# A hybrid Hyena and attention layer on one core: all gate pairs in the Strassen stage, hyena branch products beside the attention

## The chip, the core and the metric

The kernel runs on one core of a Trainium2 chip. The core has a matrix engine (TensorE, PE in the profile, with its weight loads as PEld), VectorE (DVE), ScalarE (ACT), GpSimd (POOL) and a queue engine (SP) that here only issues transfers. Matrix products land in eight banks of a small accumulator memory (PSUM) and are taken from there by VectorE or ScalarE. The metric is the device time of one execution in microseconds (us), lower is better.

## What is computed

One layer of an encoder, 512 tokens of width 2048, in float32. A normalised input goes through one wide projection; its columns feed a Hyena branch (short convolutions, long convolution by transforms), an attention branch (8 query heads, 2 key/value heads) and two gates. The gated branches are added, projected and followed by a feed-forward block of width 5632.

```python
h = rms_norm(x, mix_norm_g)
proj = h @ w_in
u_h, q, k, v, g = jnp.split(proj, [c0, c1, c2, c3], axis=-1)
...
g_h, g_a = jnp.split(jax.nn.sigmoid(g + b_gate), 2, axis=-1)
merged = g_h * (y_h @ w_br_hyena) + g_a * (y_a @ w_br_attn)
x = x + merged @ w_out
h2 = rms_norm(x, ffn_norm_g)
return x + (jax.nn.silu(h2 @ w_ffn_gate) * (h2 @ w_ffn_up)) @ w_ffn_down
```

`y_h` comes from `u_h`, `y_a` from q, k and v. The gates have 2 x 2048 output channels: 16 tiles of 128 for `g_h` and 16 for `g_a`. Pair m is tile m of both. The branch products `y_h @ w_br_hyena` and `y_a @ w_br_attn` also have 16 tiles of 128 channels each, with a depth of 1024 (8 blocks).

## The kernel before

Activations lie with channels on the 128 partitions and the 512 tokens along the free side; a tile of 128 channels is `[128, 512]`. To keep float32 accuracy every operand is split into a high and a low part (ACT copies the high part, DVE subtracts to get the low one), and a plain product is three matmuls (`mm3`): high by high, high by low, low by high.

**Weights** come from one packed array `wpk` in the order of use (`weight_blocks`, L61), in tiles of eight 128x128 blocks. `wblk` (L162) loads a tile through SP's queue, and ACT (`wh`, L175) and DVE (`wl`, L176) split it; two raw and three split tiles can be in flight. `group` (L186) makes one output tile of 128 channels from n input tiles: n steps of three matmuls, each followed by a call of `step()`. A gate tile has 16 steps, a branch product 8.

**Side work.** `step()` advances a queue of generators, one at a time (`side`). A generator emits a piece of work and yields the number of steps until its next piece. The attention is such a generator, `attend_gen` (L676): it waits `Q_WAIT` (25 and 26) steps, transposes four heads, then goes through eight units `u` in which `scores` (matmuls, softmax on DVE and ACT), `turn` (transposes of the probabilities into `pt`, split by ACT and DVE) and `values` (matmuls `av`) follow each other with one or two steps in between. The steps of the plain products are thus the filler between the pieces of attention. `flush()` drains the queue without filler.

**Order around the change.** After the key/value chunk, `chunk("q0")` makes four heads of queries (64 steps, four PSUM banks), `norm_rope` normalises and rotates them (ACT, DVE, POOL) and the first attention is queued. Then gate pair 0 (2 x 16 steps), the second q chunk, the second attention queued, gate pairs 1 and 2 (`gate_pair`, L753: result through sigmoid, stored to DRAM as `gd`), and the first three hyena products (`HYENA_FIRST`), which stay in their banks. `flush()` follows. The inputs of the branch products, `yhs` and `yas`, are split into the space of the normalised input `xg`.

The **branch loop** (L1005 on) goes over m = 0 to 15. For m < 3 it multiplies both branch products with the stored gates (`gr` loaded from `gd` through ACT's queue) and stores the merged tile `md`. For the others `b_out` copies a product out (ACT, `bt`) and stores it to DRAM as `bd` through POOL's queue. Behind the iterations m = 3 to 10 stand the preparations of the Strassen stage: `x_rows` loads two tiles of x (ACT's queue) and `x_sums` forms seven sums `V[p]`, p = 0 to 7; for p < 5 `x_split` splits them at once into `X`.

The **Strassen stage** (`seven`, `run`) makes two output tiles per group with seven products instead of eight. Each product is eight 512-wide matmuls and eight 256-wide ones (a high and a low part of the weights against split sums). ACT and DVE form and split the weight sums. Here the groups are the gate pairs 3 to 15; `gate_finish` (L1034) applies the sigmoid, loads the branch product (`br` from `bd`, ACT's queue), multiplies, adds the pair and stores `md`. Behind the last group `m_first` has the first three `md` tiles loaded; the projection `o` follows.

Most waits and instruction orders are made by a scheduler: each engine has one stream in a fixed order, in which TensorE's instructions keep the order of the code, and the other engines' instructions may be set earlier than the code has them. Temporaries `tmp` share five buffers.

Of the kernel before, what the change touches and what calls it, by code (L numbers as in the profile page):

```python
# [17 lines left out]
P = 128  # L18
S = 512
D = 2048  # L20
KT = D // P
HW = 1024
HT = HW // P
# [4 lines left out]
HD = 128  # L28
EPS = 1e-6
BLK = 8  # L30
GATES_AHEAD = 3
HYENA_FIRST = 3
MLP_WAIT = 26
Z_WAIT0 = 16
N_WARM = 10
# [14 lines left out]
C_X0, C_X1, C_HV, C_Q, C_KV, C_GH, C_GA = 0, 1024, 2048, 3072, 4096, 4608, 6656  # L50
# [10 lines left out]
def weight_blocks():  # L61

    def cols(name, c0, nk, k0=0, w=P):
        return [(name, (k0 + k) * P, c0, w) for k in range(nk)]

    def gates(m):
        return cols("w_in", C_GH + m * P, KT) + cols("w_in", C_GA + m * P, KT)

    out = []
    for q in range(NQ):  # L70
        pr = [cols("w_in", c0 + c * P, KT) for c in (2 * q, 2 * q + 1) for c0 in (C_X1, C_HV)]
        out += [b for col in (pr if q else zip(*pr)) for b in col]
        for c in (2 * q, 2 * q + 1):
            out += cols("w_in", C_X0 + c * P, KT)
    for c0, m in ((C_KV, None), (C_Q, 0), (C_Q + 512, 1), (None, 2)):
        out += cols("w_in", c0, KT, w=512) if c0 is not None else []
        out += gates(m) if m is not None else []
    for m in range(HYENA_FIRST):
        out += cols("w_br_hyena", m * P, HT)
    for m in range(KT):  # L80
        out += cols("w_br_hyena", m * P, HT) if m >= HYENA_FIRST else []
        out += cols("w_br_attn", m * P, HT)

    def quarters(name, c0, c1, k0=0):
        for half, c in ((0, c0), (0, c1), (1, c1), (1, c0)):
            out.extend((name, (k0 + k) * P, c, P) for k in range(half, KT, 2))

    for m in range(GATES_AHEAD, KT):
        quarters("w_in", C_GH + m * P, C_GA + m * P)
    for k in range(KT):  # L90
        out += [("w_out", k * P, m * P, P) for m in range(WIDE)]
    for m in range(WIDE, KT):
        out += cols("w_out", m * P, KT)
    for j in range(0, FT, 2):
        for name in ("w_ffn_gate", "w_ffn_up"):
            quarters(name, j * P, (j + 1) * P)
    for f0 in (0, NSTD + KT):
        for m in range(KT):
            for f in STD_ORDER:
                out += cols("w_ffn_down", m * P, 1, k0=f0 + f)  # L100
        for m in range(0, KT, 2):
            quarters("w_ffn_down", m * P, (m + 1) * P, f0 + NSTD)
    return out


def layer_kernel(tc, wpk, xT, par, flt, zemb, w4, decT, tbl, tb2, rope, qkg, out):
    nc = tc.nc
# [12 lines left out]
    def ps_tile(name):  # L120
        return banks["pool"].tile([P, S], F32, tag="ps", bufs=banks["n"], name=name)
# [12 lines left out]
    def step():  # L134
        side["n"] += 1
        if side["wait"] > 0:
            side["wait"] -= 1
            return
        if side["cur"] is None:
            if not side["queue"]:  # L140
                return
            side["cur"] = side["queue"].popleft()
        try:
            side["wait"] = (next(side["cur"]) or 1) - 1
        except StopIteration:
            side["cur"] = None

    def flush():
        while side["cur"] is not None or side["queue"]:
            side["wait"] = 0  # L150
            step()

    def queue(gen):
        side["queue"].append(gen)

    def tmp(name):
        return tpool.tile([P, S], F32, tag="tmp", bufs=5, name=name)
# [4 lines left out]
    def wblk(nb=1):  # L162
        st = state
        if st["pos"] >= BLK:
            i = st["tile"]
            raw = wpool.tile([P, BLK * P], F32, tag="raw", bufs=2, name=f"wr{i}")
            hi = wpool.tile([P, BLK * P], F32R, tag="whi", bufs=3, name=f"wh{i}")
            lo = wpool.tile([P, BLK * P], F32R, tag="wlo", bufs=3, name=f"wl{i}")
            st.update(tile=i + 1, pos=0, hi=hi, lo=lo, raw=raw)

        i, n = st["tile"] - 1, {1: XW // 2, 2: XW}.get(st["tile"], BLK)
        if st["pos"] % n == 0:
            c = slice(st["pos"] * P, (st["pos"] + n) * P)
            nc.sync.dma_start(st["raw"][:, c], wpk[i, :, c])
            nc.scalar.copy(st["hi"][:, c], st["raw"][:, c])  # L175
            nc.vector.tensor_tensor(st["lo"][:, c], st["raw"][:, c], st["hi"][:, c].bitcast(F32), ALU.subtract)  # L176
        a = st["pos"] * P
        st["pos"] += nb
        return st["hi"][:, a:a + nb * P], st["lo"][:, a:a + nb * P]

    def mm3(ps, ah, al, bh, bl, first, last, **kw):
        mm(ps, ah, bh, first, False, **kw)
        mm(ps, ah, bl, False, False, **kw)
        mm(ps, al, bh, False, last, **kw)

    def group(ps, act, k0=0, k1=None):  # L186
        n = len(act)
        for k in range(k0, n if k1 is None else k1):
            wh, wl = wblk()
            mm3(ps, wh, wl, act[k][0], act[k][1], k == 0, k == n - 1)  # L190
            step()
# [8 lines left out]
    def split_row(pool, src, tag, bufs, name):  # L200

        hl = pool.tile([P, 2 * S], F32R, tag=tag, bufs=bufs, name=name)
        nc.scalar.copy(hl[:, :S], src)
        nc.vector.tensor_tensor(hl[:, S:], src, hl[:, :S].bitcast(F32), ALU.subtract)
        return hl[:, :S], hl[:, S:]
# [20 lines left out]
    def pcol(name, i=0):  # L226
        a = PC[name] + i
        return prm[:, a:a + 1]
# [40 lines left out]
    def cw(name, shape, tag, bufs=1, dt=F32):  # L269
        return cv.tile(shape, dt, tag=tag, bufs=bufs, name=name)  # L270
# [248 lines left out]
    for j in range(4):  # L519
        for lst, i in ((Th, 0), (Tl, 1)):  # L520
            t = r3.tile([P, S], F32R, tag="r", bufs=16, name=f"T{i}{j}")
# [3 lines left out]
    for j in range(2):  # L525
        t = [cw(f"CS{i}{j}", [P, S], f"cs{i}{j}", 1, F32R) for i in range(2)]
# [214 lines left out]
    for tb in range(NTB):  # L741
# [7 lines left out]
    rpq = rope_tables(0, "q")  # L749
    gd = [[dpool.tile([P, S], F32, tag=f"gd{i}{m}", bufs=1, name=f"gd{i}{m}") for m in range(GATES_AHEAD)]  # L750
          for i in range(2)]

    def gate_pair(m):  # L753
        for i in range(2):
            gp = ps_tile(f"g{i}{m}")
            group(gp, xg)
            t = tmp(f"gt{i}{m}")
            nc.vector.tensor_tensor(t, gp, rbc, ALU.mult)
            nc.scalar.activation(t, t, AF.Sigmoid, bias=pcol("bgate", i * KT + m))
            nc.gpsimd.dma_start(gd[i][m], t)  # L760

    for g in range(2):
        qr = norm_rope(chunk(f"q{g}"), 4, rpq, f"q{g}")
        queue(attend_gen(g, qr))
        gate_pair(g)
    gate_pair(2)

# [3 lines left out]
    NP = KT // 2  # L773
# [5 lines left out]
    bd = [[dpool.tile([P, S], F32, tag=f"bd{i}{m}", bufs=1, name=f"bd{i}{m}") for m in range(KT)] for i in range(2)]  # L779
# [192 lines left out]
        return x_sums, x_split, V, run, lambda: raws["fold"]  # L972


    yhs = [split_row(r1, t, "hl", 16, f"yhs{i}") for i, t in enumerate(yh)]
    bps = [ps_tile(f"b0{m}") for m in range(HYENA_FIRST)]
    for bp in bps:
        group(bp, yhs)
    flush()
    ats.release()  # L980
    at.release()
# [11 lines left out]
    def x_rows(k):  # L993
        t = tmp(f"xg{k}")
        nc.scalar.dma_start(t, xT[k])
        nc.vector.tensor_tensor(t, t, rbc, ALU.mult)
        return t

    def b_out(i, m, bp):
        t = tmp(f"bt{i}{m}")  # L1000
        nc.scalar.copy(t, bp)
        nc.gpsimd.dma_start(bd[i][m], t)

    lastb = []
    for m in range(KT):  # L1005
        gs = []
        for i, src in enumerate((yhs, yas)):
            if m < GATES_AHEAD:
                gs.append(tmp(f"gr{i}{m}"))
                nc.scalar.dma_start(gs[i], gd[i][m])  # L1010
            if i == 0 and m < HYENA_FIRST:
                bp = bps[m]
            else:
                bp = ps_tile(f"b{i}{m}")
                group(bp, src)
            if m < GATES_AHEAD:
                nc.vector.tensor_tensor(gs[i], bp, gs[i], ALU.mult)
            elif m < KT - 1:
                b_out(i, m, bp)
            else:  # L1020
                lastb.append((i, m, bp))
        if m < GATES_AHEAD:
            nc.vector.tensor_tensor(gs[0], gs[0], gs[1], ALU.add)
            nc.gpsimd.dma_start(md[m], gs[0])
        elif m >= GATES_AHEAD and m - GATES_AHEAD < NP:
            p = m - GATES_AHEAD
            V[p] = x_sums(p, x_rows(2 * p), x_rows(2 * p + 1))
            if p < NEARLY:
                x_split(p, V[p], (0, 7))
# [170 lines left out]
    for half, f0 in enumerate((0, NSTD + KT)):  # L1200
# [3 lines left out]
        for m in range(KT):  # L1204
# [4 lines left out]
            t = t2[:, m % 2 * S:(m % 2 + 1) * S]  # L1209
            nc.vector.tensor_tensor(t, dp, rbc2, ALU.mult)  # L1210
            add_up(m, t)
            if m % 2 == 0:
                p = m // 2
# [124 lines left out]
```

## Time and profile before

| what | us |
| --- | --- |
| median of 3 runs | 2559.84 (2558.88 to 2561.92) |
| the profiled execution's own time | 2558.89 |
| its span | 2557.1 |
| first q chunk | 406.5 to 451 |
| gate pair 0 and second q chunk | 451 to 549.3 |
| gate pairs 1 and 2 | 549.3 to 618.4 |
| three early hyena products | 618.4 to 643.9 |
| rest of the branch loop | 643.9 to 801.6 |
| Strassen stage of the gates | 801.6 to 1063 |
| output projection, feed-forward block | 1063 to the end |

The profile is one execution on the chip. A view by stretches gives, for each engine, the busy us and (after x) the number of instructions, then the granted clock of TensorE as a share of full speed, the share of the transfer engines and GB/s. A timeline row has the start, the duration, the engine, the line of the code, the operation and `output<-inputs`, and in brackets the idle time of the engine before it and what ended it; `ACTq` is a transfer issued by ACT. A row of the chain has the start, the duration and the matmuls merged into it. A row of groups has busy us and mean ns behind the first bar. A few per cent of the matmul records are missing, so counts of matmuls come from the code.

### The profile page before, as it was taken

Reading aid. Unit: us, or ns where it says so; the run is one execution under the profiler, and the core shown is the slowest. Engines: PE = TensorE matmul, PEld = TensorE weight load, DVE = VectorE, ACT = ScalarE, POOL = GpSimd, SP = SyncE. Lnnn points to the kernel's source line nnn. Section 1 sums busy time; section 2 is a strip of 40 time slices with the busy share of each in tenths; the row PEclk is TensorE's granted clock in tenths of the full one; section 3 lists DMA queues with packets and bytes.
Section 4 is the critical chain, followed back from the end, with each engine's and each line's share of the span. In section 5 each row is a group of like instructions: output and inputs, shape, how many; then the busy total and the mean of one; then the engine's idle time right before and its main releaser. Section 6 shows DMA issues by size and latency. Waiting matters only on the chain.

```text
span 2557.1 us, 35161 instructions
## 1 busy us (share of the span) xinstructions
PE 2537.2 (99%) x13426; PEld 2180.9 (85%) x13426; DVE 2018.2 (79%) x2915; ACT 1192.0 (47%) x1781; POOL 176.7 (7%) x291
## 2 busy tenths in 40 slices
PE   9999999999999999999999999999999999999999
PEld 7888888888887888888788888888888888888888
DVE  7878763757555999754799888898889888998897
ACT  6544433546343444543544444444444445445443
POOL 1000011110010000000000000000000002001111
PEclk9999999999999999999999999999999999999999
DMA  7323333223453444544233333333333339547654
GB/s 243 107 97 105 104 112 107 76 78 108 163 185 135 163 141 149 194 156 147 99 118 118 122 124 116 132 116 123 117 132 111 129 125 234 166 130 185 177 157 116
DMA packets 112901, 346.27 MB, mean 135 GB/s; under 512 B 13851, under 2 KB 15131, under 8 KB 112508
## 3 DMA queue, kind: packets, MB, share of 16 engines
q1 hardware_dynamic: 70128, 248.02, 27.8%
q0 software_dynamic: 22192, 59.00, 8.9%
q10 hardware_dynamic: 20412, 37.01, 4.6%
q8 instruction: 105, 1.72, 0.3%
q14 instruction: 64, 0.52, 0.1%
HBM read 295.47 MB, written 52.17 MB: 136 GB/s over the span
## 4 chain that ended last, share of the span: by engine, by line
PE 72%; issue 22%; DVE 3%; POOL 1%; ACT 1%; DMA 1%; POOLq 0%; ACTq 0%; DVEq 0%; SPq 0%
PE fx L124 8%; PE px L124 7%; PE o L124 7%; PE b L124 7%; PE gx L124 6%; PE fy L124 4%; PE dx L124 3%; PE q L124 3%; PE ex L124 3%; PE gy L124 3%; PE d L124 3%; PE phv L124 2%; PE fz L124 2%; PE kv L124 2%; PE dy L124 2%
## 5 line engine op out<-in xcount | busy, mean ns | idle before, releaser
L176 DVE TENSOR_TENSOR wl<-wr,wh 128x1024 fp32r<-128x1024 f32 (+1 forms) x176 | 210.9, 1199 | 171.1 <-ACT wh L175 170.4
L175 ACT CAST wh<-wr 128x1024 fp32r<-128x1024 f32 (+1 forms) x176 | 181.9, 1033 | 298.1 <-PE o L124 65.8
L857 ACT CAST fwhs<-fs 128x1024 fp32r<-128x1024 f32 x176 | 185.0, 1052 | 237.0 <-PE fx L124 112.3
L857 ACT CAST fwha<-fa 128x1024 fp32r<-128x1024 f32 x132 | 138.8, 1052 | 206.4 <-PE fx L124 105.5
L858 DVE TENSOR_TENSOR fwls<-fs,fwhs 128x1024 fp32r<-128x1024 f32 x176 | 214.8, 1221 | 7.1 <-ACT fwhs L857 0.6
L124 PE MATMUL fx<-fX,fwhs 128*128 128x512 f32 x704 | 178.1, 395 | 3.2 <-DVE fv L873 3.2
L124 PE MATMUL px<-xh,wh 128*128 128x512 f32 x576 | 180.0, 394 | 0.0
L124 PE MATMUL fx<-fX,fwha 128*128 128x512 f32 x704 | 177.0, 393 | 1.2 <-DVE fX L825 1.1
L124 PE MATMUL fy<-fX,fwhs 128*128 128x512 f32 x704 | 176.5, 392 | 0.0
L858 DVE TENSOR_TENSOR fwla<-fa,fwha 128x1024 fp32r<-128x1024 f32 x132 | 161.2, 1221 | 3.9 <-ACT fwha L857 0.5
L124 PE MATMUL o<-ms,wh 128*128 128x512 f32 x512 | 157.6, 389 | 0.0
L124 PEld LDWEIGHTS fx<-fX,fwhs 128*128 128x128 f32 x704 | 127.7, 190 | 26.5 <-DVE fv L873 3.5
L124 PEld LDWEIGHTS fx<-fX,fwha 128*128 128x128 f32 x704 | 126.7, 189 | 24.6 <-DVE fX L825 1.7
L124 PEld LDWEIGHTS fy<-fX,fwhs 128*128 128x128 f32 x704 | 126.6, 189 | 22.6
L124 PEld LDWEIGHTS px<-xh,wh 128*128 128x128 f32 x576 | 106.1, 189 | 23.1 <-issue 2.4
L124 PE MATMUL d<-act,wh 128*128 128x512 f32 x384 | 118.2, 389 | 0.0
L124 PEld LDWEIGHTS o<-ms,wh 128*128 128x128 f32 x512 | 96.0, 188 | 19.9
L124 PE MATMUL px<-xh,wl 128*128 128x512 f32 x288 | 112.5, 391 | 0.0
L850 DVE TENSOR_TENSOR fs<-fa,fa 128x1024 f32<-128x1024 f32 x88 | 107.1, 1217 | 1.2 <-DMA fa<-wpk 0.9
L850 DVE TENSOR_TENSOR fs<-fs,fa 128x1024 f32<-128x1024 f32 x88 | 107.0, 1216 | 0.0
L124 PEld LDWEIGHTS fx<-fX,fwls 128*128 128x128 f32 x704 | 96.7, 192 | 7.0
L124 PEld LDWEIGHTS fy<-fX,fwls 128*128 128x128 f32 x704 | 96.1, 190 | 6.9
(1097 smaller groups left out, 5995.5 us busy)
## 6 DMA issues: line engine op xcount, KB each, us to landing
fa<-wpk SPq DMA_DIRECT2D x176, 512.0 KB, 3.5
wr<-wpk SPq DMA_DIRECT2D x170, 512.0 KB, 3.5
ga<-wpk SPq DMA_DIRECT2D x52, 512.0 KB, 3.5
da<-wpk SPq DMA_DIRECT2D x32, 512.0 KB, 4.4
ea<-wpk SPq DMA_DIRECT2D x32, 512.0 KB, 4.2
actd<-c POOLq DMA_DIRECT2D x41, 256.0 KB, 4.4
actr<-actd ACTq DMA_DIRECT2D x41, 256.0 KB, 4.5
x2d<-dt POOLq DMA_DIRECT2D x32, 256.0 KB, 5.1
```

What stands on the lines that cost most here:

```text
L124: tc.keep_in_program_order(nc.tensor.matmul(out, lhsT=lhsT, rhs=rhs, start=start, stop=stop, **kw))
L175: nc.scalar.copy(st["hi"][:, c], st["raw"][:, c])
L176: nc.vector.tensor_tensor(st["lo"][:, c], st["raw"][:, c], st["hi"][:, c].bitcast(F32), ALU.subtract)
L850: nc.vector.tensor_tensor(t, a, b, ALU.add)
L857: nc.scalar.copy(hi, w)
L858: nc.vector.tensor_tensor(lo, w, hi.bitcast(F32), ALU.subtract)
```

## The change

The constant `GATES_AHEAD` goes from 3 to 0: no gate pair is made by plain products, and the Strassen stage makes all 16. The second q chunk stands directly behind the first. `HYENA_FIRST` becomes `range(15)`: fifteen hyena products stand where three stood, each copied out at once by `b_out`, which moves up for that. The branch loop keeps 16 attention products and one hyena product; the preparations of the Strassen stage stand behind m = 0, 2, 4, 6, 8, 10, 12 and 13 (`x_at`). The packed weights follow the new order.

```diff
-GATES_AHEAD = 3
-HYENA_FIRST = 3
+GATES_AHEAD = 0
+HYENA_FIRST = range(15)
...
-    for c0, m in ((C_KV, None), (C_Q, 0), (C_Q + 512, 1), (None, 2)):
-        out += cols("w_in", c0, KT, w=512) if c0 is not None else []
-        out += gates(m) if m is not None else []
-    for m in range(HYENA_FIRST):
+    for c0, m in ((C_KV, None), (C_Q, 0), (C_Q + 512, None)):
+        out += cols("w_in", c0, KT, w=512)
+        out += gates(m) if m is not None and m < GATES_AHEAD else []
+    for m in HYENA_FIRST:
         out += cols("w_br_hyena", m * P, HT)
     for m in range(KT):
-        out += cols("w_br_hyena", m * P, HT) if m >= HYENA_FIRST else []
+        out += cols("w_br_hyena", m * P, HT) if m not in HYENA_FIRST else []
         out += cols("w_br_attn", m * P, HT)
...
         queue(attend_gen(g, qr))
-        gate_pair(g)
-    gate_pair(2)
+        if g < GATES_AHEAD:
+            gate_pair(g)
...
+    def b_out(i, m, bp):
+        t = tmp(f"bt{i}{m}")
+        nc.scalar.copy(t, bp)
+        nc.gpsimd.dma_start(bd[i][m], t)
+
     yhs = [split_row(r1, t, "hl", 16, f"yhs{i}") for i, t in enumerate(yh)]
-    bps = [ps_tile(f"b0{m}") for m in range(HYENA_FIRST)]
-    for bp in bps:
+    for m in HYENA_FIRST:
+        bp = ps_tile(f"b0{m}")
         group(bp, yhs)
+        b_out(0, m, bp)
     flush()
...
     lastb = []
+    x_at = {m: p for p, m in enumerate((0, 2, 4, 6, 8, 10, 12, 13))}
     for m in range(KT):
         gs = []
         for i, src in enumerate((yhs, yas)):
+            if i == 0 and m in HYENA_FIRST:
+                continue
+            bp = ps_tile(f"b{i}{m}")
+            group(bp, src)
             if m < GATES_AHEAD:
                 gs.append(tmp(f"gr{i}{m}"))
                 nc.scalar.dma_start(gs[i], gd[i][m])
-            if i == 0 and m < HYENA_FIRST:
-                bp = bps[m]
-            else:
-                bp = ps_tile(f"b{i}{m}")
-                group(bp, src)
-            if m < GATES_AHEAD:
                 nc.vector.tensor_tensor(gs[i], bp, gs[i], ALU.mult)
             elif m < KT - 1:
                 b_out(i, m, bp)
...
-        elif m >= GATES_AHEAD and m - GATES_AHEAD < NP:
-            p = m - GATES_AHEAD
+        p = x_at.get(m)
+        if p is not None:
             V[p] = x_sums(p, x_rows(2 * p), x_rows(2 * p + 1))
```

More of the change, by code (lines that the diff above doesn't have):

```diff
@@ L997, in x_rows @@
         return t
[L999 to L1002, printed above, removed]
     lastb = []
+    x_at = {m: p for p, m in enumerate((0, 2, 4, 6, 8, 10, 12, 13))}
     for m in range(KT):
```

## The prediction, on record before the changed kernel ran

> **What bounds the kernel now.** I read the page first, then the busy time by stretches, then the chain.
>
> ```profile
> span 2557.1 us, 35161 instructions
> PE 2537.2 (99%) x13426; PEld 2180.9 (85%) x13426; DVE 2018.2 (79%) x2915; ACT 1192.0 (47%) x1781; POOL 176.7 (7%) x291
> PE 72%; issue 22%; DVE 3%; POOL 1%; ACT 1%; DMA 1%; POOLq 0%; ACTq 0%; DVEq 0%; SPq 0%
> ```
>
> TensorE is busy for 99% of the span, and the chain that ended last is TensorE's own work. So an edit is worth what it takes from the sum of matmuls, plus or minus the waits of TensorE that it removes or makes. The stretches below are, in order: gate pair 0 with the second q chunk; gate pairs 1 and 2; the three early hyena products; the branch loop; entry into the Strassen stage; the rest of that stage.
>
> ```profile
> core 0: us, PE busy (x) PEld busy (x) DVE busy (x) ACT busy (x) POOL busy (x), PEclk, DMA share, GB/s
> 451.00:549.30 98.30, 97.75 (x514) 82.87 (x513) 62.03 (x131) 48.89 (x125) 10.15 (x18) 1.00 0.20 70
> 549.30:618.40 69.10, 69.00 (x365) 58.62 (x365) 56.89 (x127) 50.87 (x114) 11.94 (x19) 1.00 0.22 74
> 618.40:633.50 15.10, 13.11 (x80) 10.82 (x79) 8.64 (x19) 7.92 (x15) 0.54 (x1) 1.00 0.67 242
> 643.90:801.60 157.70, 157.70 (x697) 130.61 (x696) 74.18 (x90) 67.38 (x93) 15.11 (x28) 1.00 0.47 165
> 801.60:823.00 21.40, 17.38 (x84) 14.30 (x84) 19.34 (x19) 8.83 (x12) 0.54 (x1) 0.84 0.48 172
> 823.00:1063.00 240.00, 239.94 (x1375) 210.98 (x1375) 218.67 (x296) 119.17 (x161) 6.48 (x12) 1.00 0.43 151
> ```
>
> TensorE idles in two places only: 2.0 us (15.10 less 13.11) in 618.4 to 633.5, and 4.0 us at the entry, where the granted clock is 0.84. Everywhere else here a matmul saved is time saved.
>
> **Term 1: three gate pairs move from plain matmuls into the Strassen stage.** In plain groups the weight tiles give the beat: one tile of eight blocks is eight steps of three 512-wide matmuls. The first two rows are ACT's timeline in the branch loop, the next three the chain at the same product of three successive Strassen groups.
>
> ```profile
> 655.01 1.05 ACT L175 CAST wh<-wr 128x1024 fp32r<-128x1024 f32 x1 [4.43 <-PE b L124]
> 660.45 1.05 ACT L175 CAST wh<-wr 128x1024 fp32r<-128x1024 f32 x1 [4.39 <-PE b L124]
> ```
>
> ```profile
> 842.60 2.79 PE gz L124 x16
> ...
> 862.15 2.79 PE gz L124 x16
> ...
> 881.71 2.79 PE gz L124 x16
> ```
>
> A tile is 5.44 us, a step 0.68 us, a matmul 0.227 us. A gate pair is 2 x 16 steps, four tiles: 21.76 us; three are 65.28 us. A Strassen group, which makes one pair, is (881.71 - 842.60) / 2 = 19.55 us, or seven products of 2.79; three more are 58.66 us. The term is 58.66 - 65.28 = **-6.6 us**. It has no cover to lose: in 823 to 1063 TensorE fills 239.94 of 240.00 us. The next engine is VectorE with 218.67, 17.8 us of each 19.55, so it does not take over. Weight bytes are the same (four tiles a pair either way). Each new group adds two loads of `br` on ACT's queue and one store of `md` on POOL's, and drops two `gd` stores and two `gr` loads; ACT has 119 busy us in 240, so I cost these at nothing; `md` 0 to 2, which the last group preloads, are then written thirteen groups earlier. If that cover were gone, the late thing would be `gate_finish`, with a group of slack.
>
> **Term 2: twelve hyena products as filler.** They leave the branch loop (12 tiles, 65.28 us) and stand where three gate pairs stood (12 tiles, 65.28 us), so the sum is zero and only TensorE's waits can change. Counting yields: the first attention generator resumes on step 26 and issues its last `values` on step 69; the second takes 70 more, its last on step 140. Behind the first q chunk there are 184 steps before and after (32+64+32+32+24, then 64+120). Now the second generator is queued at step 96 and ends on the sixth hyena step; then it is queued at 64, starts at 71 and ends on the 76th hyena step. Both stay covered.
>
> **Term 3: the tail of the second attention.** The last two `turn`s have one step between transposes and `values`. The timeline there:
>
> ```profile
> 623.42 0.40 PE L124 MATMUL b<-yhs,wl 128*128 128x512 f32 x1
> 624.30 0.39 PE L124 MATMUL av<-pt160sh,vh 128*128 128x256 f32 x1 [0.48 <-ACT pt160sh L196]
> 624.68 4.34 ACTq L1010 DMA_DIRECT2D gr<-gd  x2
> 625.03 0.39 PE L124 MATMUL av<-pt160sl,vh 128*128 128x256 f32 x1 [0.34 <-DVE pt160sl L197]
> ...
> 628.48 0.40 PE L124 MATMUL b<-yhs,wl 128*128 128x512 f32 x1
> 629.07 0.59 ACT L196 CAST pt170sh<-pt 128x512 fp32r<-128x512 f32 x1 [3.81 <-DMA gd<-gt]
> 629.70 0.39 PE L124 MATMUL av<-pt170sh,vh 128*128 128x256 f32 x1 [0.82 <-ACT pt170sh L196]
> 630.43 0.38 PE L124 MATMUL av<-pt170sl,vh 128*128 128x256 f32 x1 [0.34 <-DVE pt170sl L197]
> ```
>
> Starts are 0.227 us apart behind a 512-wide matmul and 0.12 behind a 256-wide one. So 624.30 is 0.65 late, 625.03 0.61, 629.70 0.99, 630.43 0.61: 2.9 us. ACT stood at a `gr` load that waited for the `gd` store of the last gate; no `gr` and `gd` are left in the changed kernel. The first attention's tail shows the same place without that:
>
> ```profile
> 524.89 0.28 PE L124 MATMUL av<-pt060sh,vh 128*128 128x256 f32 x1
> 525.38 0.39 PE L124 MATMUL av<-pt060sl,vh 128*128 128x256 f32 x1 [0.21 <-DVE pt060sl L197]
> ...
> 529.07 0.28 PE L124 MATMUL av<-pt070sh,vh 128*128 128x256 f32 x1
> 529.55 0.39 PE L124 MATMUL av<-pt070sl,vh 128*128 128x256 f32 x1 [0.21 <-DVE pt070sl L197]
> ```
>
> That is 0.37 + 0.36 = 0.7 us; with a weight or `yas` cast in between I take 0.9. The term is **-2.0 us**, between 0 (another ACT instruction stands there) and -2.2.
>
> **Term 4: the end of the second q chunk.** Steps 65 to 69 (`values` 5, `turn` 6, `values` 6, `turn` 7, `values` 7) now fall behind the chunk, where `norm_rope` of q1 also wants ACT and VectorE. Before, nothing of an attention was running there. Its work, by groups from 547 to 569 us, and its longest block:
>
> ```profile
> L657 POOL TENSOR_TENSOR q1o<-q1qn,rpq 128x128 f32<-128x128 f32 x16 | 10.3, 678 | 78.5 <-ACT q1qn L647 78.5
> L655 DVE TENSOR_TENSOR q1t<-q1qn,rpq 128x128 f32<-128x128 f32 x16 | 6.0, 431 | 0.0
> L647 ACT ACTIVATE q1qn<-q,q1ry 128x128 f32<-128x128 f32 x16 | 4.3, 389 | 1.8 <-DVE q1o L658 1.8
> ...
> L211 ACT ACT_TABLE_LOAD x1 | 1.3, 1283 | 0.0
> ```
>
> ```profile
> 552.72 1.28 ACT L211 ACT_TABLE_LOAD   x1
> 554.01 0.22 ACT L211 ACTIVATE q1rt<-q1ss 128x16 f32<-128x16 f32 x1
> 554.77 1.05 ACT L175 CAST wh<-wr 128x1024 fp32r<-128x1024 f32 x1 [0.54 <-PE g L124]
> 555.73 3.20 ACT L647 ACTIVATE q1qn<-q,q1ry 128x128 f32<-128x128 f32 x12
> 560.72 1.15 ACT L647 ACTIVATE q1qn<-q,q1ry 128x128 f32<-128x128 f32 x4 [1.80 <-DVE q1o L658]
> ```
>
> ACT and VectorE run their streams in order, so a `pt` cast can stand behind the 1.28 us table load or the 3.20 us block of scalings, with `values` on TensorE behind it and all later matmuls behind that. If no cast meets one, the cost is 0. If turn 6 meets half the table load (0.6) and turn 7 nearly half the block (1.4), it is 2 us, on top of the 0.7 that this tail costs already. If everything of the norm stands ahead, see the slower rival. I take **+2.0 us**, near the lower end: the chunk's last row of steps is stretched by attention work, so the squares of three of the four token blocks run before its end, and the cast at 554.77 shows that later work was set between the norm's pieces, not behind them. The banks allow it: the chunk holds four, and the score tiles are out before `turn` 6 asks for two.
>
> The Trainium skill ("ScalarE: Activation LUTs", "What ACT_TABLE_LOAD costs") adds a drain of about 1.38 us to each 1.28 us load; by it this term would be an estimated 3.4 us. The rows show no drain: the load of 552.72 ends at 554.00 and its activation starts at 554.01. I keep 2.0.
>
> **Term 5: the sums for the Strassen entry come later.** The loop has 17 groups instead of 29; the last `x_sums` follows the attention product m = 13, three groups (16.3 us) ahead of the entry. How long it takes is seen at the first one, whose group ended at 671.2 us:
>
> ```profile
> 671.52 0.82 ACTq L995 DMA_DIRECT2D xg<-xT  x2
> ...
> 678.41 1.70 ACT L824 CAST gX<-gV 128x1792 fp32r<-128x1792 f32 x1
> ```
>
> V is ready 7.2 us after its group; behind the pair of m = 12, one group ahead, I allow 3 more. 10 of 16.3 us: cost 0. `yhs` and `yas` splits need rows of the normalised input to come free, which happens during the second q chunk, where VectorE and ACT have room (62.03 and 48.89 of 98.30). The fifteen `bt` stores go out on POOL behind up to 10.3 us of rotary products; they hold only `tmp` tiles, and the banks are copied out by ACT.
>
> **The sum**, against the profiled execution's 2558.89 us (1.79 outside the span): -6.6 + 0 - 2.0 + 2.0 + 0 = -6.6, so 2552.3 us. The median of the runs is 0.95 above that execution, which gives 2553.2; I take the middle, **2552.8 us**.
>
> **The rivals.**
> - *No collision.* Term 4 is zero: 2558.89 - 8.6 = 2550.3. For it: casts were set between the norm's pieces before. Against it: one step of 0.68 us is all the slack those casts have. 14%.
> - *The norm ahead of the casts (slower).* Its calls are written ahead of the hyena groups in whose steps turns 6 and 7 are issued. If their casts and subtractions stand behind all of it, to about 567 us in the old trace, 18 us behind the chunk's end at 549.3, `values` 6, due 4.5 us behind it, waits 13.5 us: -8.6 + 13.5 = +4.9, 2563.8. It decides from a wait of 8.6 us. Against it: the weight casts between. 8%.
> - *Half of that*, some 5 us of waits: -3.6, 2555.3. 13%.
> - *The clock drops at the new waits.* At the entry, waits went with a granted clock of 0.84 over 21.40 us, 3.4 us of lost clock. Here that gives -6.6 + 3.4 = -3.2, 2555.7. Against it: the waits of 618 to 633 left it at 1.00. 5%. The Trainium skill ("TensorE: Matmul & The Clock Gate", "What's actually happening") has the clock halved after an idle window of about 3.4 us; the trace agrees as far as it goes: the 4.0 us of idle time at the entry went with a drop, the 2.0 us of 618 to 633 did not.
> - *V late at the entry.* Fourteen us instead of ten cost nothing, twenty cost 4: -2.6, 2556.3. 4%.
>
> **How the numbers follow.** The forecast has 56%, with waits of term 4 from 0.5 to 4 us: 2550.8 to 2554.3 by the profiled execution, 0.95 more by the median. A measurement here tells about 0.2%, 5.1 us, so the bound is 2554.7. Forecast less its slow edge (48%) and no collision (14%) are faster: 0.62. That edge (8%) and the three middle rivals (22%) are within: 0.30. Slower: 0.08. The range goes from 1.8 us under the no-collision case to 1.2 over the late-V case: 2548.5 to 2557.5.
>
> **What would show it.** Sixteen Strassen groups of 19.55 us; no `gr` rows; waits of `av` for pt16 and pt17 under 1 us; waits of `av` for pt06 and pt07, now on hyena filler, of 2 to 3 us in all; the entry wait for gX near 4 us. A group longer than 19.55, waits of `av` above 5 us behind the second q chunk, or an entry that waits for V would make me wrong.

## The result, and the profile after

The changed kernel takes **2565.53 us** (median of 14 runs, 2562.59 to 2569.24) against 2560.44 us (14 runs) before: a ratio of 1.002 with a 95% interval of 1.0013 to 1.0028. It is slower, by about 5 us (0.2%); 2552.8 us was forecast. The profiled execution took 2562.59 us, 3.7 us more than that of before. First the page of the changed kernel:

```profile
span 2560.8 us, 35336 instructions
PE 2531.4 (99%) x13474; PEld 2179.4 (85%) x13474; DVE 2048.7 (80%) x2960; ACT 1201.7 (47%) x1804; POOL 175.3 (7%) x291
```

TensorE is busy for 5.8 us *less* than before (2537.2), in a span that is 3.7 us longer. So its sum of work fell and its waits rose. The stretches show where; they are: second q chunk, the 24 us behind its end, hyena filler with most of the second attention, the end of that attention with the rest of the filler and the branch loop, the Strassen entry, the Strassen stage.

```profile
451.00:521.00 70.00, 69.11 (x366) 58.59 (x364) 57.27 (x125) 43.84 (x124) 9.02 (x16) 1.00 0.18 61
521.00:545.00 24.00, 13.91 (x73) 11.59 (x72) 16.86 (x46) 13.39 (x39) 9.69 (x16) 0.79 0.07 23
545.00:612.00 67.00, 67.00 (x356) 57.14 (x355) 38.78 (x81) 33.27 (x65) 4.37 (x8) 1.00 0.28 95
612.00:748.00 136.00, 135.42 (x622) 112.54 (x621) 70.90 (x93) 67.11 (x99) 12.41 (x23) 1.00 0.50 170
748.00:769.50 21.50, 17.19 (x87) 14.32 (x86) 19.78 (x21) 8.06 (x11) 0.54 (x1) 0.92 0.54 178
769.50:1067.00 297.50, 297.26 (x1703) 261.35 (x1702) 271.17 (x366) 149.13 (x201) 8.10 (x15) 1.00 0.44 150
```

One stretch is out of line: the 24 us behind the second q chunk, where TensorE is busy for 13.91 us and the granted clock is 0.79. What it waited for, from 451 to 830 us (us in total, times, longest):

```profile
PE av L124 <- DVE pt070sl L197: 4.6, 1, 4.6
PE av L124 <- ACT pt070sh L196: 4.3, 1, 4.3
PE gx L124 <- DVE gX L825: 4.3, 3, 1.4
PE qT00p L127 <- DVE q0o L658: 0.9, 1, 0.9
PE av L124 <- ACT pt060sh L196: 0.7, 1, 0.7
PE av L124 <- DVE pt060sl L197: 0.5, 1, 0.5
PE av L124 <- DVE pt160sl L197: 0.4, 1, 0.4
...
PE av L124 <- DVE pt170sl L197: 0.2, 1, 0.2
```

Two single waits, both of `values` 7 of the first attention, hold 9 us. The timeline there, with TensorE, ACT and VectorE in one order of time:

```profile
526.53 1.06 ACT L175 CAST wh<-wr 128x1024 fp32r<-128x1024 f32 x1
527.47 0.63 ACT L203 CAST yas<-ya 128x512 fp32r<-128x512 f32 x1
529.05 3.20 ACT L647 ACTIVATE q1qn<-q,q1ry 128x128 f32<-128x128 f32 x12 [0.94 <-DVE q1ry L641]
529.15 1.03 PE L127 MATMUL pt<-ident,p 128*128 128x128 f32 x8
...
530.49 0.40 PE L124 MATMUL b<-yhs,wl 128*128 128x512 f32 x1
...
533.55 1.14 ACT L647 ACTIVATE q1qn<-q,q1ry 128x128 f32<-128x128 f32 x4 [1.30 <-DVE q1o L658]
534.57 0.60 ACT L196 CAST pt070sh<-pt 128x512 fp32r<-128x512 f32 x1
535.22 0.58 PE L124 MATMUL av<-pt070sh,vh 128*128 128x256 f32 x1 [4.34 <-ACT pt070sh L196]
...
538.85 0.94 DVE L655 TENSOR_TENSOR q1t<-q1qn,rpq 128x128 f32<-128x128 f32 x3
539.72 0.68 DVE L197 TENSOR_TENSOR pt070sl<-pt,pt070sh 128x512 fp32r<-128x512 f32 x1
540.45 0.58 PE L124 MATMUL av<-pt070sl,vh 128*128 128x256 f32 x1 [4.65 <-DVE pt070sl L197]
...
542.96 1.05 PE L124 MATMUL b<-yhs,wh 128*128 128x512 f32 x2
...
545.47 0.63 PE L124 MATMUL b<-yhs,wh 128*128 128x512 f32 x2
```

Turn 7's transposes are out at 530.2. Its cast stands on ACT behind the last four scalings of `norm_rope` of q1, which themselves waited 1.30 us for VectorE, and starts at 534.57. Its subtraction stands on VectorE behind nearly all rotary products and sums of the norm (the last of them at 538.85), and starts at 539.72. By the starts, 535.22 is 4.5 us late and 540.45 is 5.1 us late. The clock is low from 535.2 on, behind the first of the two waits; the second lies within the slow stretch:

```profile
535.20:545.40 10.20, 5.53 (x18) 4.76 (x19) 7.09 (x14) 1.66 (x3) 4.04 (x8) 0.50 0.01 2
```

From 540.45 to 542.96 eleven 256-wide matmuls start, 2.51 us instead of 1.32; from there to 545.47 six 512-wide ones, 2.51 instead of 1.36: 2.3 us lost. With 1.5 us at pt06 the tail of the first attention costs 13.4 us, where it cost 0.7.

### The profile page after: what moved, and what is told of

It is laid out like the page before. It is cut to its first block, busy times and chain, and to the rows that moved or that the text cites. A ratio compares the mean times of both kernels' runs of the same rounds, so it can differ in the third digit from the quotient of the medians.

```text
span 2560.8 us, 35336 instructions
## 1 busy us (share of the span) xinstructions
PE 2531.4 (99%) x13474; PEld 2179.4 (85%) x13474; DVE 2048.7 (80%) x2960; ACT 1201.7 (47%) x1804; POOL 175.3 (7%) x291
## 4 chain that ended last, share of the span: by engine, by line
PE 96%; DVE 3%; ACT 1%; issue 0%; POOL 0%; POOLq 0%; DVEq 0%; ACTq 0%
PE fx L124 19%; PE fy L124 9%; PE px L124 7%; PE gx L124 7%; PE o L124 7%; PE b L124 7%; PE d L124 5%; PE fz L124 5%; PE dx L124 3%; PE gy L124 3%; PE ex L124 3%; PE q L124 3%; PE phv L124 2%; PE ey L124 2%; PE dy L124 2%; PE gz L124 2%
## 5 line engine op out<-in xcount | busy, mean ns | idle before, releaser
L176 DVE TENSOR_TENSOR wl<-wr,wh 128x1024 fp32r<-128x1024 f32 (+1 forms) x164 | 196.2, 1198 | 160.4 <-ACT wh L175 155.6
L175 ACT CAST wh<-wr 128x1024 fp32r<-128x1024 f32 (+1 forms) x164 | 169.1, 1032 | 271.6 <-PE o L124 65.7
L857 ACT CAST gwhs<-gs 128x1024 fp32r<-128x1024 f32 x64 | 67.1, 1051 | 76.3 <-PE gx L124 37.7
```

The lines of the kernel that those rows point to most:

```text
L857: nc.scalar.copy(hi, w)
```

## The experiments

A stage mark helps to compare: the first matmul of the projection `o`, which starts when the Strassen stage ends. It is 1063.1 us before and 1067.4 us in the changed kernel. All ratios are against the kernel before, measured beside each kernel.

**The first hyena product written ahead of the norm** (`e1_product_ahead_of_norm`). The last turns come first in the code, the norm later.

```diff
-        qr = norm_rope(chunk(f"q{g}"), 4, rpq, f"q{g}")
-        queue(attend_gen(g, qr))
...
+        qps = chunk(f"q{g}")
+        if g:
...
+            for m in HYENA_FIRST[:1]:
+                hyena(m)
+        queue(attend_gen(g, norm_rope(qps, 4, rpq, f"q{g}")))
```

`hyena(m)` is the body of the loop over `HYENA_FIRST`; `yhs` is split ahead of it, and the loop behind the chunks goes on with the second product.

> The changed kernel with one edit: the first hyena product (8 steps) is written ahead of norm_rope of q1, so the last two turns of the first attention come ahead of the norm in the order of the code. Theory A (order): the casts and subtractions of turn 7 stood behind norm work in the fixed streams of ACT and VectorE; waits of av for pt06 and pt07 fall from 11.1 us and 1.4 us of slow clock to 0.7 to 1.5 us, time 2565.5 - 11.5 = 2554 (2552.5 to 2555.5). Theory B (load): ACT, VectorE and POOL have too much work in these 20 us in any order; the wait moves to the transposes of the second attention or stays, and the time falls by less than 4 us, to 2562 or more. Theory C (the three Strassen groups bring less than 6.6 us): waits go, but the time stays above 2557.

Measured: 2557.43 us, ratio 0.999 (0.9981 to 0.9999), first `o` at 1059.0. The waits of TensorE from 451 to 700 us:

```profile
PE qT10p L127 <- DVE q1o L658: 2.3, 1, 2.3
PE qT00p L127 <- DVE q0o L658: 0.9, 1, 0.9
PE av L124 <- DVE pt060sl L197: 0.4, 1, 0.4
...
PE av L124 <- DVE pt070sl L197: 0.2, 1, 0.2
```

The waits of `av` for pt06 and pt07 are gone but for 0.6 us, as theory A had it, and a part came back where theory B looked for it: the transposes of the second attention (`qT10`) now wait 2.3 us for the norm that starts later, and the clock falls to half behind them. (The 1.4 us of slow clock that the expectation starts from are 2.3 by the starts above.) The time lies between those of A and B. Theory C's time, above 2557, was met, but not its condition, as these waits are still there. Two later runs, with a longer wait of the second attention, separate the theories.

**One gate pair plain, between the chunks** (`e2_one_plain_gate_pair`).

```diff
-GATES_AHEAD = 0
-HYENA_FIRST = range(15)
+GATES_AHEAD = 1
+HYENA_FIRST = range(1, 12)
```

> The changed kernel with gate pair 0 made plainly again, between the two q chunks, and eleven hyena products (1 to 11) as filler: 32 + 64 + 88 steps. The first attention ends inside the second q chunk, as before. Theory A: no collision, two pairs in the Strassen stage instead of three more: 2560.4 - 4.4 - 2.0 = 2554.0 (2552.5 to 2556). Theory B: the same, it only speaks of the stretch behind the chunk. Theory C: 2558 or more, as the Strassen term is missing; 15 groups of clearly more than 19.55 us.

Measured: 2555.92 us, 0.9977 (0.9968 to 0.9986), first `o` at 1058.1. With the first attention ending inside the second q chunk again there is no collision, and the mark is 5.0 us earlier than in the kernel before. From the first matmul of the first q chunk to the Strassen stage it takes 350.2 us, before 395.1: 44.9 less, of which two plain gate pairs are 43.5 and the balance of the waits 1.4. The stage takes 301.1 us, before 261.2: 39.9 more, of which two groups are 39.1; where the other 0.8 goes is not known.

**Fifteen steps behind turn 7 of the first attention** (`e3_steps_in_the_tail`).

```diff
-                yield T_WAIT
+                yield T_WAIT if g or u < 8 else 15
```

> The changed kernel with 15 steps instead of 1 between turn 7 and values 7 of the first attention: 14 steps of hyena filler, 9.5 us, in the same order of the code. Theory A: TensorE works through the filler while the casts stand behind the norm; the 9.6 us of waits for pt07 and the slow clock go, the 1.5 us at pt06 stay: 2565.5 - 10.5 = 2555 (2553.5 to 2557). Theory B: the filler's weight casts and copies stand behind the norm as well, and TensorE waits for those: 2560 or more.

Measured: 2556.17 us, 0.9978 (0.9969 to 0.9987), first `o` at 1057.0. Turn 7's cast still stands behind the norm, but TensorE has filler meanwhile:

```profile
PE qT00p L127 <- DVE q0o L658: 0.9, 1, 0.9
PE av L124 <- ACT pt060sh L196: 0.7, 1, 0.7
PE av L124 <- DVE pt060sl L197: 0.4, 1, 0.4
...
PE av L124 <- DVE pt071sl L197: 0.2, 1, 0.2
```

The two long waits and the low clock are gone. So the engines have room for this work; what was short was TensorE's distance from it.

**The chunks adjacent, nothing else**, in the kernel before (`e4_chunks_adjacent_alone`; the packed weights follow the order):

```diff
         queue(attend_gen(g, qr))
-        gate_pair(g)
-    gate_pair(2)
+    for m in range(GATES_AHEAD):
+        gate_pair(m)
```

> The kernel before with one edit: the second q chunk directly behind the first, the three plain gate pairs behind it, then three hyena products. Nothing moves to the Strassen stage. Theory A: the end of the first attention meets norm_rope of q1 here too; about +10 to +12 us, 2571 (2568 to 2574), with av waiting for pt07 on ACT and VectorE. Rival D (the copies and stores of the hyena products make the wait, not the place of the chunk): 2560 to 2562.

Measured: 2571.68 us, 1.0043 (1.0027 to 1.0058), first `o` at 1073.6, 10.5 us later than before. The waits (its lines are one further down):

```profile
PE av L125 <- DVE pt070sl L198: 4.6, 1, 4.6
...
PE av L125 <- ACT pt070sh L197: 3.3, 1, 3.3
PE av L125 <- ACT pt060sh L197: 0.7, 1, 0.7
PE av L125 <- DVE pt060sl L198: 0.4, 1, 0.4
```

With gates as filler and no hyena copies the same waits appear. Rival D falls: it is the place of the chunk.

**Slack at all last turns** (`e5_slack_in_both_tails`).

```diff
-                yield T_WAIT
+                yield T_WAIT if u < 7 else 3 if g else (4, 15)[u - 7]
```

> As e3_steps_in_the_tail, with slack at each of the last turns: first attention 4 steps behind turn 6 and 15 behind turn 7, second attention 3 behind both. Theory A (fixed order and too short a countdown): the 1.5 us at pt06, 0.6 at pt07 and 0.7 of the second tail go: 2556.2 - 2.8 = 2553.4 (2552 to 2555.5). Theory B (load): a wait of the same size shows at the next piece, at the transposes qT10 of the second attention: 2555.5 or more.

Measured: 2552.36 us, 0.9967 (0.9955 to 0.9979), first `o` at 1053.4. No wait of the size came up elsewhere: beside the entry, the list of waits from 451 to 830 us has 0.9 us for `qT00` and 0.2 for pt071, and nothing for `qT10`.

**The same, first attention two steps later** (`e6_slack_and_later_start`: `Q_WAIT` 27 instead of 25).

> As e5_slack_in_both_tails, with the first attention waiting 27 steps instead of 25 behind the first q chunk. Theory A: the 1.0 us wait of the transposes qT00 goes too: 1 us under e5. Against it: two more steps push turn 5 and the exponentials of scores 7 behind the second chunk, into the norm's work; then av or pt waits 1 us or more and it is not under e5.

Measured: 2566.24 us, 1.0017 (1.0008 to 1.0026), first `o` at 1066.3: the objection was right, by 13 us and not by one. The wait of `qT00` did go, and these came:

```profile
PE av L124 <- DVE pt060sl L197: 4.2, 1, 4.2
PE av L124 <- ACT pt060sh L196: 3.3, 1, 3.3
```

ACT's timeline shows why:

```profile
527.06 3.22 ACT L647 ACTIVATE q1qn<-q,q1ry 128x128 f32<-128x128 f32 x12
530.52 1.14 ACT L647 ACTIVATE q1qn<-q,q1ry 128x128 f32<-128x128 f32 x4 [0.24 <-DVE q1o L658]
531.68 1.28 ACT L700 ACT_TABLE_LOAD   x1
532.98 0.69 ACT L700 ACTIVATE p<-sp,sm 128x512 f32<-128x512 f32 x1
...
534.32 0.58 ACT L196 CAST pt060sh<-pt 128x512 fp32r<-128x512 f32 x1
```

Now the exponentials of scores 7 and the casts of turn 6 are behind the norm, and the four steps in front of `values` 6 do not cover them; the fifteen behind turn 7 stand at the wrong place.

**The norm late, and a longer wait of the second attention** (`e7_norm_late_longer_wait`: the first experiment with `Q_WAIT` 32 instead of 26 for the second attention).

> As e1_product_ahead_of_norm, with the second attention waiting 32 steps instead of 26. There the transposes qT10 waited 2.4 us for the norm's last rotary sums and 1.4 us went to the slow clock behind it. Theory A: this was the countdown, too short for a norm that starts later; it goes: 2557.4 - 3.8 = 2553.6 (2552 to 2555.5). Theory B (the engines are over-full in this stretch): half of it or more stays, 2555.5 or more.

Measured: 2552.98 us, 0.9969 (0.9956 to 0.9981), first `o` at 1055.1. The wait of `qT10` is gone, so it was the countdown, not the load.

**That, with slack** (`e8_norm_late_and_slack`: `Q_WAIT` 26 and 32, two steps behind turns 6 and 7 of both).

> As e7_norm_late_longer_wait, with 26 steps for the first attention and 2 steps behind turns 6 and 7 of both. Theory A: the remaining 0.9 us of the first tail and 0.7 of the second shrink, qT00 by 0.7: 2 us under e7, 2551.6 (2550.5 to 2553.5), the no-collision sum of the prediction. Theory C (Strassen term smaller than 6.6): stays above 2554 with the waits gone.

Measured: **2551.31 us**, 0.9961 (0.9948 to 0.9973), first `o` at 1052.6. It beats both kernels: by the ratios it stands 10 us under the one before (7 to 13), and the changed one 5 us above. All waits of TensorE of 0.2 us or more from 451 to 830 us that are left:

```profile
PE gx L124 <- DVE gX L838: 4.0, 3, 1.4
PE qT00p L127 <- DVE q0o L658: 0.2, 1, 0.2
PE gx L124 <- ACT gwhs L870: 0.2, 1, 0.2
```

**Adjacent chunks and slack, gates still plain** (`e9_adjacent_plain_gates_with_slack`: the fourth kernel with the edit of the fifth).

> As e4_chunks_adjacent_alone (the three gate pairs plain, as filler behind the second q chunk, three hyena products, thirteen Strassen groups) with the slack of e5_slack_in_both_tails. It differs from e5 only in what the change moves: three gate pairs to the Strassen stage, twelve hyena products up. Theory A: its waits fall to those of e5, and e5 stands 6.6 us under it; so about 4 us under the kernel before (waits 10.3 us down to some 7): ratio 0.9985 (0.997 to 0.9995) against 0.9967 of e5 with 2.6 thousandths between. Theory C (the three Strassen groups bring less): the two stand within 3 us of each other, about 0.1%.

Measured: 2557.8 us, 0.9991 (0.9982 to 1.0), first `o` at 1060.1. The stage marks of this kernel and of the one with slack at all last turns, in that order (the second pair of times is the first and last start):

```profile
L125 PE MATMUL o<-ms,wh x512: 389/389/397, 1060.1 to 1233.8; 128*128 128x512 f32 x171
```

```profile
L124 PE MATMUL o<-ms,wh x512: 389/389/397, 1053.4 to 1227.0; 128*128 128x512 f32 x171
```

The two differ only in what goes to the Strassen stage and in the filler: 6.7 us. From the first matmul of the first q chunk to the stage they take 391.9 and 326.7 us, 65.2 less (three plain pairs are 65.28); the stage takes 262.1 and 320.5, 58.4 more (three groups are 58.66). The ratios, 0.9991 and 0.9967, say 6 us, and their intervals (0.9982 to 1.0 and 0.9955 to 0.9979) do not overlap. Theory C, which had the two within 3 us, falls.

## Why the prediction was wrong

**Term 1, the Strassen groups: right.** The chain of the changed kernel at the same product of the second and the last group:

```profile
788.22 2.79 PE gz L124 x16
...
1061.96 2.79 PE gz L124 x16
```

Fourteen groups in 273.74 us are 19.55 us each, as forecast, and the pair of kernels above gives 6.7 us for a term of 6.6.

**Term 2, the filler: right in its sum.** Twelve hyena products cover as many steps as three gate pairs. Its copies and stores make no wait of TensorE in the list above.

**Term 3, the second tail: right.** The subtractions of turns 6 and 7 make `values` 0.59 and 0.31 us late by the starts (619.47 and 623.57), 0.9 in all where 0.9 was taken; before it was 2.9.

**Term 4, the end of the second chunk: the step that failed.** It was priced at 2.0 us and is 13.4 - 0.7 = 12.7. The case that came is the slower rival, the norm ahead of the casts, which had 8%. That its price of 13.5 us comes so near is chance: it is one wait of `values` 6 at full clock, and what came are 1.5 us at `values` 6, 9.6 at `values` 7 and 2.3 of slow clock. The prediction's own sign of being wrong, waits of `av` above 5 us behind the second q chunk, is there: 10.1 us in the list. Three things went wrong in the step:

- It priced "nearly half the block" of ACT's scalings. ACT's part alone was 4.3 us: the block comes in two pieces, and the second waits for a rotary sum of VectorE.
- It left out VectorE, although the rows were there: 6.0 us of `q1t` and the sums, whose other terms are 10.3 us of POOL (VectorE waits 1.58 us for POOL ahead of the first sum, at 532.59). The subtraction stood behind them, and TensorE waited 4.6 us more.
- The clock was kept as a rival of its own and not added to the case of long waits, where it belongs: 2.3 us.

The argument for the low price was a weight cast set between the norm's pieces. It shows that work which is ready in a gap of the norm is set there; the rows of after show `wh` and `yas` in that very gap at 526.53 and 527.47. Turn 7's transposes came at 529.15, 0.1 us behind the start of the block. The question to ask was when the casts become ready, not whether gaps exist: the counted steps gave it (turn 7 on step 68, four steps behind the chunk).

**Term 5, the entry: right.** The waits for gX are 4.3 us (4.0 before). From its first product (747.4) to the first `o` the stage takes 320.0 us, 7.2 more than sixteen groups; before (from 801.9) it took 261.2, 7.0 more than thirteen.

**Not in the sum:** the transposes `qT00` wait 0.9 us for the last rotary sum of q0, some 0.7 more than before. It is the same fault in small. In VectorE's stream a weight subtraction now stands ahead of that sum, where a gate's product of 0.68 us stood before:

```profile
468.10 1.21 DVE L176 TENSOR_TENSOR wl<-wr,wh 128x1024 fp32r<-128x1024 f32 x1
469.23 0.68 DVE L658 TENSOR_TENSOR q0o<-q0o,q0t 128x512 f32<-128x512 f32 x1
```

Together: -6.6 (term 1), -2.0 (term 3), +12.7 (term 4), +0.7 (`qT00`) make +4.8. The stage mark moved by +4.3, or by +4.7 counted from the first matmul of the first q chunk (406.8 before, 406.4 after), and the medians by +5.1.

## What to carry to other kernels

Before moving a stretch of work next to another, list for *each* engine with a fixed order what will stand ahead of the small pieces that the bounding engine waits for, and when these become ready. A place that hides twenty us of side work costs nothing until a short dependence lands in it; the cure is distance for the waiting engine (steps of filler) or an earlier place in the code, and neither needs less work. A countdown in steps holds for one neighbourhood only: two steps more cost 13 us here.

## What was not expected of the hardware

The clock fell to 0.50 behind a wait of 4.5 us and stayed there for 10.2 us, in which the second wait, of 5.1 us, lies. In the first experiment a single wait of 2.3 us was enough. The row of that kernel behind it:

```profile
554.70:558.10 3.40, 3.40 (x12) 2.71 (x12) 1.68 (x2) 0.59 (x1) 0.00 (x0) 0.52 0.99 314
```

The Trainium skill ("TensorE: Matmul & The Clock Gate", "What's actually happening") puts the drop behind an idle window of about 3.4 us. The lengths of the slow stretches agree with such a window (3.4 us here, three times that in the changed kernel); that 2.3 us of waiting is enough does not follow from it. At the Strassen entry no single wait is above 1.4 us, and the granted clock falls there too (0.84 in 801.6 to 823.0 before, 0.92 in 748.0 to 769.5 after). Waits of 0.8 and 0.7 us in a row at pt06 left the clock at 1.00 in the third experiment.
